# Score pieces of the A and B prompt attention put on TensorE two at a time, with four score banks and two shared by values and transposes

## The chip, the cores and the metric

One core of one Trainium2 chip. The metric is the device time of one execution in microseconds; three runs are taken and their median is told. TensorE is PE in the profile (PEld its weight loads), VectorE DVE, ScalarE ACT, GpSimd POOL and SyncE SP, the queue that issues most DMAs.

## What is computed

One layer of a streaming encoder, on 1024 prompt rows and 8 x 16 sample rows of width 1024. Three branches read one input projection; their outputs are gated, merged and followed by a feed-forward block. The change touches the prompt's part of branches A (a band of 64-row chunks with a bias by distance, 8 heads of 64) and B (causal, with a forget gate in the logits, 8 heads of 64), and, through the banks, the memory branch M and the sample rows:

```python
qa, ka, va, qb, kb, vb, logf, qm, gates = project(xn, ...)
# A: every 64-row chunk of queries reads its own and 8 earlier chunks
s = jnp.einsum('bcqhd,bckhd->bchqk', qc, kband) * d ** -0.5 + rel_bias
o_a = jnp.einsum('bchqk,bckhd->bcqhd', softmax(where(valid, s, -inf)), vband)
# B: every query reads all keys up to itself
s = jnp.einsum('bqhd,bkhd->bhqk', qi, k) * scale + ci[..., :, None] - c[..., None, :]
o_b = jnp.einsum('bhqk,bkhd->bqhd', softmax(where(k_pos <= q_pos, s, -inf)), v)
h = sigmoid(g_a) * (o_a @ w_pa) + sigmoid(g_b) * (o_b @ w_pb) + sigmoid(g_m) * (o_m @ w_pm)
x = x + h @ w_o
x = x + (relu(rmsnorm(x) @ w_up) ** 2) @ w_down
```

## The kernel before, in words

Values in float32 that need more than one TensorE pass are split into a high and a low part, and a product is three matmuls: high by high, high by low, low by high. The program runs through the input projection (to about 410 us), the attention stages with other products between them (to about 1100 us), the rest of the merge, and then W_o and the feed-forward block (to the end).

The attention stages run one after the other, each a call of `attend` (L1798 to L1807): prompt A, samples A, prompt B, samples B, prompt M, samples M. In each a generator yields tasks, and `Plan.run` (L148) decides on the order in which they are put on the engines. A task is a pair `ready` and `emit` with a chain's name. The planner keeps a clock of its own for PE (`plan.now`) and estimates for the other engines; it looks at the first 12 tasks, emits the first whose `ready()` is not after its clock, one chain's tasks in order, and where none is ready it takes one step of a filler, `plan.fill` (L135). The filler (`gates`, then `merge`) is the gate and merge products, matmuls on the whole 128 x 128 array into the two banks `z`. What is emitted is kept in program order on each engine, so the chip runs the order that the planner made.

PSUM has eight banks, given out by kind (L1777): two for filler (`z`), two for transposes (`tp`), three for scores (`s`), one for values (`pv`). `plan.bank(k, m)` tells when m banks of a kind are free by the planner's estimate, `take` and `free` keep its books.

`prompt_ab` (L1091) handles both branches. Heads go in pairs p, queries in blocks of 128, and n = 0 to 31 counts blocks over the four pairs (A upwards from block 0, B downwards from block 7). For each n:

- `scores` (L1161) cuts the block's keys into pieces of up to 512 columns: one piece up to 512 keys, two above. For A the number of keys is 128, 256, 384, 512 and then 640 (384 + 256) for blocks 0 to 7, for B 128 to 1024. A piece is a task (L1193): it takes two banks, one per head, and issues six matmuls, three terms by two heads. The two heads stand in the upper and lower 64 rows of the array (`tile_position`), and run side by side. `soften` (L1174) is the eviction: one VectorE instruction adds the bias and finds the row's extreme, and frees the bank; behind the last piece come the exponential on ACT and the scaling by DVE or POOL.
- `transposes` (L1214) turns the probabilities of n - 2 by PE into the `tp` banks; ACT or DVE copies them out as `pt`.
- `values` (L1258), for every second n, multiplies them with V into the `pv` bank, the two heads in the two column halves of the array; `os` is the copy on its way to HBM.

The sample stages use the array in four column strips of 32 (`s<-kd,qb`, `pv<-vd,spt`); their keys `kd` and values `vd` come from HBM through SP's queue. So the array is used whole (filler, transposes, M), by row halves (scores of A and B), by column halves (values of A and B) or by column strips (samples).

Of the kernel before, what the change touches and what calls it, by code (L numbers as in the profile page):

```python
# [187 lines left out]
def tile_encoder(ctx: ExitStack, tc: tile.TileContext, i, o):  # L188
# [902 lines left out]
    def prompt_ab(b, pool):  # L1091
# [69 lines left out]
        def scores(n):  # L1161
# [31 lines left out]
            def piece(x, m):  # L1193
                def ready():
                    return max(kq[p], bias_at[2 * p], bias_at[2 * p + 1], plan.bank("s", 2),
                               0.0 if x or 2 * n + 2 - softs[0] <= NS else INF)

                def emit():
                    qh, ql, kh, kl = heads[p][:4]
                    ks, qc, ps = slice(k0 * P + x, k0 * P + x + m), slice(blk * P, (blk + 1) * P), []  # L1200
                    for e in range(2):
                        if x == 0:
                            ss_[n, e] = tl(pool, (P, WK), tag="s", bufs=NS)
                        ps.append((plan.take("s"), tl(psum["s"], (P, 512), tag="s")))
                    for j, (q, k) in enumerate(((qh, kh), (qh, kl), (ql, kh))):
                        for e in range(2):
                            r = slice(64 * e, 64 * e + 64)
                            pe.matmul(ps[e][1][:, :m], q[r, qc], k[r, ks], start=j == 0, stop=j == 2, tile_position=(64 * e, 0))
                    for e in range(2):
                        plan.spawn(soften(e, ps[e][1], ps[e][0], x, m, x + m == nkey))  # L1210
                return ready, emit
            return [(*piece(x, m), ("s", n)) for x, m in pieces]
# [45 lines left out]
        def values(n):  # L1258
# [23 lines left out]
            def ready():  # L1282
                return max([vb[p], plan.bank("pv")] + [summed[x].get(e, INF) for x in (n - 1, n) for e in range(2)])

            def emit():
                bk = plan.take("pv")
                pv, vd = tl(psum["pv"], (P, 512), tag="pv")[:, 0:256], heads[p][4]
# [12 lines left out]
        plan.spawn(biases())  # L1300
        for n in range(32 + 4):
# [4 lines left out]
            if n < 32:  # L1306
                yield from scores(n)

    def prompt_m(pool):
# [98 lines left out]
        def values(n):  # L1408
# [11 lines left out]
            def ready():  # L1420
                return max(at["l", n], at["l", n - 1], at["in", 0], plan.bank("pv"))

            def emit():
                bk = plan.take("pv")
# [335 lines left out]
    def begin(gen):  # L1760

        for t in gen:
            plan.t = max(plan.t, t)
# [484 lines left out]
```

## Time and profile before

| | |
|---|---|
| median of 3 runs | 2029.59 us (2027.34 to 2035.56) |
| profiled execution, its own time | 2028.52 us |
| span of its trace | 2026.7 us |
| PE busy | 1968.0 us, 97% |
| DVE busy | 1233.7 us, 61% |
| ACT busy | 942.6 us, 47% |
| POOL busy | 524.8 us, 26% |

The profiled execution is 1.8 us longer than its span, and 1.1 us below the median. Matmuls are pipelined: a matmul's length in the trace runs into the next one's, so what one costs the queue is read from the distance of two starts. Time with nothing to wait for that the profile shows stands as "issue". Line numbers are those of the kernel before; L203 and L215 are the helpers that issue every ACT, DVE, POOL or SP instruction and every matmul, L222 the transposes.

### The profile page before, as it was taken

To read this page: it belongs to the slowest core of one execution; us is meant where nothing else is said; L and a number is where in the kernel's file an instruction comes from. 1 tells how busy PE (TensorE), PEld (TensorE's weight loads), DVE (VectorE), ACT (ScalarE), POOL (GpSimd) and SP (SyncE) were. 2 spreads that over 40 slices of the span, in tenths; PEclk is the share of its full clock that TensorE was granted. 3 is DMA by queue.
4 is the path that set the end of the run, shared out by engine and by line. 5 is a ranking of instruction groups with operands and counts; after the bars stand their busy time and mean duration, and the time that the engine had idled before them with its cause. 6 is when DMAs were issued, how large, how long until landed. Compare 5 with 4: busy or idle time off the path is not lost. (4 is left out here: it accounts for less than half of the span.)

```text
span 2026.7 us, 33952 instructions
## 1 busy us (share of the span) xinstructions
PE 1968.0 (97%) x12338; PEld 1710.5 (84%) x12338; DVE 1233.7 (61%) x2320; ACT 942.6 (47%) x1827; POOL 524.8 (26%) x587
## 2 busy tenths in 40 slices
PE   8999999899999999999998999989999999999999
PEld 8887888777778887787897987889999997888887
DVE  7776657666523655522575752785666565785775
ACT  6645556466633455533452222554444454453332
POOL 3343424233211234311122210244444331000000
PEclk9999999999999999999998999999999999999999
DMA  8556455642278333278657553134434359663463
GB/s 265 158 157 184 117 169 159 204 131 92 78 217 281 118 102 107 67 237 280 189 187 270 154 162 110 58 125 162 145 126 147 131 167 321 188 201 106 129 195 127
DMA packets 223910, 330.54 MB, mean 163 GB/s; under 512 B 32358, under 2 KB 109303, under 8 KB 223743
## 3 DMA queue, kind: packets, MB, share of 16 engines
q1 hardware_dynamic: 166600, 270.44, 42.1%
q10 hardware_dynamic: 57142, 57.93, 8.7%
q8 instruction: 97, 1.59, 0.3%
q14 instruction: 71, 0.57, 0.1%
HBM read 243.11 MB, written 85.18 MB: 162 GB/s over the span
## 5 line engine op out<-in xcount | busy, mean ns | idle before, releaser
L1849 PE MATMUL b<-r 128*128 128x512 f32 (+2 forms) x2200 | 456.7, 356 | 5.8 <-DVE r L203 3.2
L1849 PEld LDWEIGHTS b<-r 128*128 128x128 f32 x2200 | 378.8, 189 | 64.1 <-DVE r L203 4.6
L203 ACT ACTIVATE r<-fa 128x512 fp32r<-128x512 f32 (+4 forms) x264 | 212.8, 816 | 327.5 <-PE b L1849 278.0
L203 DVE TENSOR_TENSOR r<-fa,r 128x512 fp32r<-128x512 f32 (+4 forms) x264 | 275.5, 1055 | 137.9 <-ACT r L203 133.7
L215 PE MATMUL z<-hi,whi 128*128 128x384 f32 x960 | 321.2, 366 | 9.4 <-ACT hi L203 4.0
L1849 PE MATMUL b<-r,r 128*128 128x320 f32 (+1 forms) x1928 | 287.5, 299 | 5.2 <-DVE r L203 5.1
L1849 PEld LDWEIGHTS b<-r,r 128*128 128x128 f32 x1928 | 270.7, 190 | 7.0 <-DVE r L203 7.0
L215 PE MATMUL z<-hi,wlo 128*128 128x384 f32 x768 | 261.5, 341 | 0.2
L203 POOL TENSOR_TENSOR fa<-fa 128x512 f32<-128x512 f32 x114 | 166.0, 1463 | 238.8 <-ACT fa L203 135.4
L215 PEld LDWEIGHTS z<-hi,whi 128*128 128x128 f32 x960 | 180.3, 192 | 42.0 <-issue 23.3
L215 PE MATMUL z<-wa,hi 128*128 128x512 f32 (+1 forms) x732 | 203.7, 365 | 6.7 <-ACT hi L203 5.0
L215 PE MATMUL z<-lo,whi 128*128 128x384 f32 x576 | 194.9, 338 | 0.0
L215 PEld LDWEIGHTS z<-wa,hi 128*128 128x128 f32 x732 | 128.8, 192 | 27.6 <-ACT hi L203 5.4
L203 ACT ACTIVATE s<-s,nm 128x256 f32<-128x256 f32 (+8 forms) x180 | 121.4, 678 | 60.4 <-DVE nm L203 58.6
L215 PEld LDWEIGHTS z<-hi,wlo 128*128 128x128 f32 x768 | 146.8, 191 | 0.9 <-DVE wlo L203 0.9
L203 POOL TENSOR_SCALAR s<-s,ri 128x256 f32<-128x256 f32 (+8 forms) x105 | 77.0, 738 | 265.8 <-DVE ri L203 219.0
L203 DVE CUSTOM_DVE_ANT_0 s<-s,bias 128x384 f32<-128x384 f32 (+4 forms) x144 | 71.0, 526 | 100.5 <-PE s L215 100.0
L215 PE MATMUL z<-wa,lo 128*128 128x512 f32 (+1 forms) x366 | 130.2, 359 | 0.0
L215 PEld LDWEIGHTS z<-lo,whi 128*128 128x128 f32 x576 | 109.9, 191 | 0.0
L222 PE MATMUL tp<-ident,s 128*128 128x128 f32 (+1 forms) x680 | 102.2, 276 | 1.2 <-POOL s L203 1.2
L203 DVE TENSOR_TENSOR fa<-b,fa 128x256 f32<-128x256 f32 (+1 forms) x160 | 70.8, 450 | 52.4 <-PE b L1849 38.1
L203 DVE TENSOR_TENSOR wa<-rw,wa 128x512 fp32r<-128x512 f32 (+1 forms) x102 | 67.8, 687 | 56.3 <-ACT wa L203 56.3
(223 smaller groups left out, 3149.2 us busy)
## 6 DMA issues: line engine op xcount, KB each, us to landing
td<-fa SPq DMA_DIRECT2D x112, 256.0 KB
rw<-in_w_in SPq DMA_DIRECT2D x104, 256.0 KB
fa<-td SPq DMA_DIRECT2D x80, 256.0 KB
fa<-in_w_down SPq DMA_DIRECT2D x76, 256.0 KB
fa<-in_w_up SPq DMA_DIRECT2D x32, 512.0 KB
tg<-tg ACTq DMA_DIRECT2D x72, 192.0 KB
th<-tg SPq DMA_DIRECT2D x72, 192.0 KB
wst<-in_w_g ACTq DMA_DIRECT2D x48, 256.0 KB
```

The lines of the kernel that those rows point to most:

```text
L203: ins = f(*a, **k)
L215: ins = nc.tensor.matmul(out, lhsT, rhs, **k)
L222: ins = nc.tensor.transpose(*a)
L1849: pin(nc.tensor.matmul(ps, lh, rh, **k))
```

## The change

A score task is now one or two pieces, `together`. Its `ready` asks for two banks per piece, so for four with two pieces, and it emits the pieces one behind the other: twelve matmuls. B puts the pieces of one block together (one or two). A gathers pieces over the blocks until there are two: blocks 0 and 1, blocks 2 and 3, and the two pieces of each further block. The banks are given out anew: four for scores, and none of its own for values, which take one of the two `tp` banks, in the prompt's and the samples' stages alike.

```diff
@@ -1190,26 +1190,35 @@
                     yield from exp_norm(s[:, :nkey], s[:, :nkey], nkey, nm, pool)
                     done[n, e] = plan.t
 
-            def piece(x, m):
-                def ready():
-                    return max(kq[p], bias_at[2 * p], bias_at[2 * p + 1], plan.bank("s", 2),
-                               0.0 if x or 2 * n + 2 - softs[0] <= NS else INF)
-
-                def emit():
-                    qh, ql, kh, kl = heads[p][:4]
-                    ks, qc, ps = slice(k0 * P + x, k0 * P + x + m), slice(blk * P, (blk + 1) * P), []
+            def begin(x, m, heads):
+
+                qh, ql, kh, kl = heads[:4]
+                ks, qc, ps = slice(k0 * P + x, k0 * P + x + m), slice(blk * P, (blk + 1) * P), []
+                for e in range(2):
+                    if x == 0:
+                        ss_[n, e] = tl(pool, (P, WK), tag="s", bufs=NS)
+                    ps.append((plan.take("s"), tl(psum["s"], (P, 512), tag="s")))
+                for j, (q, k) in enumerate(((qh, kh), (qh, kl), (ql, kh))):
                     for e in range(2):
-                        if x == 0:
-                            ss_[n, e] = tl(pool, (P, WK), tag="s", bufs=NS)
-                        ps.append((plan.take("s"), tl(psum["s"], (P, 512), tag="s")))
-                    for j, (q, k) in enumerate(((qh, kh), (qh, kl), (ql, kh))):
-                        for e in range(2):
-                            r = slice(64 * e, 64 * e + 64)
-                            pe.matmul(ps[e][1][:, :m], q[r, qc], k[r, ks], start=j == 0, stop=j == 2, tile_position=(64 * e, 0))
-                    for e in range(2):
-                        plan.spawn(soften(e, ps[e][1], ps[e][0], x, m, x + m == nkey))
-                return ready, emit
-            return [(*piece(x, m), ("s", n)) for x, m in pieces]
+                        r = slice(64 * e, 64 * e + 64)
+                        pe.matmul(ps[e][1][:, :m], q[r, qc], k[r, ks], start=j == 0, stop=j == 2, tile_position=(64 * e, 0))
+                for e in range(2):
+                    plan.spawn(soften(e, ps[e][1], ps[e][0], x, m, x + m == nkey))
+            return [(p, n, x, m, begin) for x, m in pieces]
+
+        def together(pieces):
+
+            p = pieces[0][0]
+            last = max(n for _, n, _, _, _ in pieces)
+
+            def ready():
+                return max(kq[p], bias_at[2 * p], bias_at[2 * p + 1], plan.bank("s", 2 * len(pieces)),
+                           0.0 if 2 * last + 2 - softs[0] <= NS else INF)
+
+            def emit():
+                for _, _, x, m, begin in pieces:
+                    begin(x, m, heads[p])
+            return ready, emit, ("s", last)
 
         def transposes(n):
 
@@ -1280,11 +1289,11 @@
                 store(oT[b][p * P:(p + 1) * P, g * 256:(g + 1) * 256], os, 128)
 
             def ready():
-                return max([vb[p], plan.bank("pv")] + [summed[x].get(e, INF) for x in (n - 1, n) for e in range(2)])
+                return max([vb[p], plan.bank("tp")] + [summed[x].get(e, INF) for x in (n - 1, n) for e in range(2)])
 
             def emit():
-                bk = plan.take("pv")
-                pv, vd = tl(psum["pv"], (P, 512), tag="pv")[:, 0:256], heads[p][4]
+                bk = plan.take("tp")
+                pv, vd = tl(psum["tp"], (P, 512), tag="tp")[:, 0:256], heads[p][4]
                 for m, (kb, a, z) in enumerate(plan_):
                     u, r = divmod(kb - low(g), UK)
                     for e in range(2):
@@ -1298,13 +1307,18 @@
 
         plan.spawn(prepare(0))
         plan.spawn(biases())
+        waiting = []
         for n in range(32 + 4):
             if 0 <= n - 2 < 32:
                 yield from transposes(n - 2)
             if n - 3 >= 0 and n % 2 == 0:
                 yield from values(n - 3)
             if n < 32:
-                yield from scores(n)
+                waiting += scores(n)
+
+                if len(waiting) == 2 or b == "b":
+                    yield together(waiting)
+                    waiting = []
 
     def prompt_m(pool):
         mkp = tuple(tl(pool, (P, 4, NMEM), F32R, tag=f"mk{s}", bufs=1) for s in "hl")
...
@@ -1575,11 +1589,11 @@
         def values(n):
 
             def ready():
-                return max(at["T", n, 512], at["T", n, P], at["V", n], plan.bank("pv"))
+                return max(at["T", n, 512], at["T", n, P], at["V", n], plan.bank("tp"))
 
             def emit():
-                bk = plan.take("pv")
-                pv = tl(psum["pv"], (P, 512), tag="pv")
+                bk = plan.take("tp")
+                pv = tl(psum["tp"], (P, 512), tag="tp")
                 for k in range(5):
                     for pr in range(4):
                         pe.matmul(pv[32 * pr:32 * pr + 32, 0:P], pts[n][k][:, 32 * pr:32 * pr + 32], vv[n][k][:, pr * P:(pr + 1) * P],
...
@@ -1774,7 +1788,7 @@
     in_order.clear()
     prj.close()
     att = ExitStack()
-    plan.bufs = dict(z=2, tp=2, s=3, pv=1)
+    plan.bufs = dict(z=2, tp=2, s=4)
     att.enter_context(banks(**plan.bufs))
 
     def fillers():
```

**On PE, prompt B, first pair of heads.** The second block's score piece in the program before and the products behind it (`s` scores of the two heads, `z` filler):

```order
L215 MATMUL s_7513<-kh_7278,qh_7280 128x512
L215 MATMUL s_7515<-kh_7278,qh_7280 128x512
L215 MATMUL s_7513<-kl_7279,qh_7280 128x512
L215 MATMUL s_7515<-kl_7279,qh_7280 128x512
L215 MATMUL s_7513<-kh_7278,ql_7281 128x512
L215 MATMUL s_7515<-kh_7278,ql_7281 128x512
L215 MATMUL z_7472<-hi_144_212,whi_7429 128x384
L215 MATMUL z_7472<-lo_151_219,whi_7429 128x384
L215 MATMUL z_7472<-hi_144_212,wlo_7430 128x384
```

The same block in the changed program:

```order
L215 MATMUL s_7603<-kh_7374,qh_7376 128x512
L215 MATMUL s_7605<-kh_7374,qh_7376 128x512
L215 MATMUL s_7603<-kl_7375,qh_7376 128x512
L215 MATMUL s_7605<-kl_7375,qh_7376 128x512
L215 MATMUL s_7603<-kh_7374,ql_7377 128x512
L215 MATMUL s_7605<-kh_7374,ql_7377 128x512
L215 MATMUL s_7612<-kh_7374,qh_7376 128x384
L215 MATMUL s_7613<-kh_7374,qh_7376 128x384
L215 MATMUL s_7612<-kl_7375,qh_7376 128x384
L215 MATMUL s_7613<-kl_7375,qh_7376 128x384
L215 MATMUL s_7612<-kh_7374,ql_7377 128x384
L215 MATMUL s_7613<-kh_7374,ql_7377 128x384
```

The six score matmuls of 512 columns are followed at once by the six of the block's second piece (384 columns), which stood twelve products further on; filler stands ahead of and behind the twelve.

**On PE, prompt A, the first group of values.** Before (`pt` turned probabilities, `vd` the values):

```order
L215 MATMUL z_4203<-hi_143_211,wlo_4031 128x384
L215 MATMUL pv_4235<-pt_4112,vd_3839 64x256
L215 MATMUL pv_4235<-pt_4113,vd_3839 64x256
L215 MATMUL pv_4235<-pt_4112,vd_3839 64x128
L215 MATMUL pv_4235<-pt_4113,vd_3839 64x128
L215 MATMUL s_4246<-kh_3835,qh_3837 128x384
L215 MATMUL s_4248<-kh_3835,qh_3837 128x384
L215 MATMUL s_4246<-kl_3836,qh_3837 128x384
L215 MATMUL s_4248<-kl_3836,qh_3837 128x384
```

In the changed program:

```order
L215 MATMUL z_4235<-lo_146_214,whi_4027 128x384
L215 MATMUL z_4235<-hi_143_211,wlo_4028 128x384
L215 MATMUL tp_4257<-pt_4113,vd_3836 64x256
L215 MATMUL tp_4257<-pt_4114,vd_3836 64x256
L215 MATMUL tp_4257<-pt_4113,vd_3836 64x128
L215 MATMUL tp_4257<-pt_4114,vd_3836 64x128
L222 MATMUL tp_4269<-ident_203,s_4129 128x128 x3
L215 MATMUL z_4235<-hi_143_211,whi_4027 128x384
L215 MATMUL z_4235<-lo_147_215,whi_4027 128x384
```

The values' output is a `tp` tile in place of `pv`, and what follows is a transpose into the other `tp` bank and filler, where a score piece followed directly.

**On SP, the loads of the A samples.** Before (`kd` keys, `vd` and `v` values):

```order
L203 DMA vd_6670<-in_cav 128x512 x4
L203 DMA kd_6694<-in_cak 128x512 x4
L203 DMA kd_6747<-in_cak 128x512 x4
L203 DMA v_1240_6344<-out_va 16x512
L203 DMA vd_6813<-in_cav 128x512 x4
L203 DMA kd_6833<-in_cak 128x512 x4
L203 DMA v_1238_6342<-out_va 16x512
```

In the changed program:

```order
L203 DMA vd_6773<-in_cav 128x512 x4
L203 DMA kd_6800<-in_cak 128x512 x4
L203 DMA kd_6850<-in_cak 128x512 x4
L203 DMA kd_6907<-in_cak 128x512 x4
L203 DMA v_1252_6447<-out_va 16x512
L203 DMA vd_6934<-in_cav 128x512 x4
L203 DMA v_1250_6445<-out_va 16x512
```

A load of keys has moved ahead of the values of a sample before it; the loads ahead of these rows stand as they did.

## Rows read from the trace of the kernel before

**Rows 1.** The page, part 1: busy time, share of the span and instructions per engine.

```profile
PE 1968.0 (97%) x12338; PEld 1710.5 (84%) x12338; DVE 1233.7 (61%) x2320; ACT 942.6 (47%) x1827; POOL 524.8 (26%) x587
```

**Rows 2.** Windows: stretch, then busy time and instructions per engine, PEclk, DMA share, GB/s.

```profile
410.00:585.00 175.00, 175.00 (x1278) 141.41 (x1277) 99.48 (x344) 102.48 (x264) 52.76 (x73) 1.00 0.36 110
...
650.00:865.00 215.00, 215.00 (x1515) 176.44 (x1506) 120.73 (x357) 113.90 (x262) 72.26 (x112) 1.00 0.32 103
865.00:965.00 100.00, 93.87 (x844) 81.67 (x841) 27.98 (x87) 31.75 (x77) 14.59 (x35) 0.98 0.82 259
```

**Rows 3.** Tile `qh`: count, min/median/max ns, first and last start, then shapes.

```profile
L215 PE MATMUL s<-kh,qh x192: 322/439/503, 410.5 to 863.6; 64*128 64x384 f32 x80, 64*128 64x256 f32 x56, 64*128 64x512 f32 x40, 64*128 64x128 f32 x16
```

**Rows 4.** Timeline of PE, 769 to 774 us: start, length, instruction.

```profile
769.17 0.60 PE L222 MATMUL tp<-ident,s 128*128 128x128 f32 x4
769.53 0.42 PE L215 MATMUL z<-hi,whi 128*128 128x384 f32 x1
...
771.17 0.38 PE L222 MATMUL tp<-ident,s 128*128 128x128 f32 x2
771.31 0.42 PE L215 MATMUL z<-hi,whi 128*128 128x384 f32 x1
771.57 0.34 PE L215 MATMUL z<-lo,whi 128*128 128x384 f32 x1
771.75 0.33 PE L215 MATMUL z<-hi,wlo 128*128 128x384 f32 x1
772.01 0.51 PE L215 MATMUL s<-kh,qh 64*128 64x512 f32 x2
772.35 0.40 PE L215 MATMUL s<-kl,qh 64*128 64x512 f32 x2
772.58 0.40 PE L215 MATMUL s<-kh,ql 64*128 64x512 f32 x2
772.92 0.44 PE L215 MATMUL z<-hi,whi 128*128 128x384 f32 x1
773.20 0.34 PE L215 MATMUL z<-lo,whi 128*128 128x384 f32 x1
773.37 0.33 PE L215 MATMUL z<-hi,wlo 128*128 128x384 f32 x1
```

**Rows 5.** Timeline of PE, 599 to 601 us, around column-tiled products.

```profile
599.04 0.34 PE L215 MATMUL z<-hi,wlo 128*128 128x384 f32 x1
599.31 1.08 PE L215 MATMUL pv<-vd,spt 128*32 128x128 f32 x32
...
600.54 0.45 PE L215 MATMUL z<-hi,whi 128*128 128x384 f32 x1
600.82 0.34 PE L215 MATMUL z<-lo,whi 128*128 128x384 f32 x1
```

**Rows 6.** Weight loads (PEld), 410 to 865 us, by line and shape; idle time at the end.

```profile
L215 PEld LDWEIGHTS z<-hi,whi 128*128 128x128 f32 x414 | 78.4, 189 | 22.6 <-issue 19.0
...
L215 PEld LDWEIGHTS s<-kh,qh 64*128 64x128 f32 x192 | 17.9, 183 | 19.9 <-issue 17.3 <-DVE pt L203 0.7 <-DVE s L203 0.5
```

**Rows 7.** Who PE waited for, 410 to 1100 us: us in total, times, longest.

```profile
PE z L215 <- ACT hi L203: 4.0, 3, 1.5
PE s L215 <- DMA kd<-in_cak: 3.4, 3, 2.6
PE s L215 <- DMA kd<-in_cmk: 2.7, 1, 2.7
```

**Rows 8.** Windows around one stall, 600 to 611 us.

```profile
607.20:610.60 3.40, 3.40 (x15) 2.62 (x10) 1.46 (x7) 0.83 (x2) 0.72 (x2) 0.50 0.93 348
```

**Rows 9.** DVE, 410 to 865 us, by line and shape: score evictions.

```profile
L203 DVE CUSTOM_DVE_ANT_0 s<-s,bias 128x512 f32<-128x512 f32 x32 | 20.8, 689 | 26.1 <-PE s L215 26.1
...
L203 DVE CUSTOM_DVE_ANT_0 s<-s,bias,nm 128x512 f32<-128x512 f32 x8 | 5.7, 749 | 5.5 <-PE s L215 5.5
```

**Rows 10.** ACT, 410 to 865 us, by line and shape: the values' eviction.

```profile
L203 ACT ACTIVATE os<-pv 128x256 f32<-128x256 f32 x25 | 9.6, 384 | 32.2 <-PE pv L215 32.2
```

More of the change, by code (lines that the diff above doesn't have):

```diff
@@ L1420, in ready @@
             def ready():
-                return max(at["l", n], at["l", n - 1], at["in", 0], plan.bank("pv"))
+                return max(at["l", n], at["l", n - 1], at["in", 0], plan.bank("tp"))
             def emit():
-                bk = plan.take("pv")
-                pv = tl(psum["pv"], (P, 512), tag="pv")
+                bk = plan.take("tp")
+                pv = tl(psum["tp"], (P, 512), tag="tp")
                 mm3(pv, lambda k: tuple(m[:, k, h * P:(h + 1) * P] for m in mvp),
@@ L1577, in ready @@
             def ready():
-                return max(at["T", n, 512], at["T", n, P], at["V", n], plan.bank("pv"))
+                return max(at["T", n, 512], at["T", n, P], at["V", n], plan.bank("tp"))
             def emit():
-                bk = plan.take("pv")
-                pv = tl(psum["pv"], (P, 512), tag="pv")
+                bk = plan.take("tp")
+                pv = tl(psum["tp"], (P, 512), tag="tp")
                 for k in range(5):
@@ L1716, in emit @@
             def emit():
-                bk = plan.take("pv")
-                pv = tl(psum["pv"], (P, 2, P), tag="pv")
+                bk = plan.take("tp")
+                pv = tl(psum["tp"], (P, 2, P), tag="tp")
                 for e in range(2):
@@ L1725, in emit @@
                 plan.spawn(out(pv, bk))
-            return lambda: max(at["t", n], at["v", 2 * n], at["v", 2 * n + 1], plan.bank("pv")), emit, ("v", n)
+            return lambda: max(at["t", n], at["v", 2 * n], at["v", 2 * n + 1], plan.bank("tp")), emit, ("v", n)
         def turn(n):
```

## The prediction

> **What bounds the kernel now.** I read the page's busy times first: TensorE is busy for 97% of the span, the next engine, VectorE, for 61% [rows 1]. A share of 97% can still hide stages with other limits, so the windows come next. The two stretches in which the changed code runs are the prompt's A attention (410 to 585 us) and B attention (650 to 865 us). In both PE is busy for the whole length, 175.00 of 175.00 and 215.00 of 215.00 us, at full granted clock, with DVE at 57% and 56% and the DMA engines at about a third [rows 2]. So these 390 us are set by TensorE alone: what shortens its queue shortens them. The list of who waited for whom says the same. Over 410 to 1100 us it has only twelve entries for PE, the largest 4.0 us in total; none of them lies inside the two windows, and none is a score matmul waiting for a bank that VectorE still held. The waits stand in the sample and memory stages, mostly for keys from HBM [rows 7].
>
> A busy PE is not a PE at its peak, and the timeline shows what the busy time contains [rows 4]. Inside a run of whole-array products, starts are 0.17 to 0.18 us apart for 384 columns. Around a score piece they are not. I read the starts one after the other, for a piece of 512 columns whose two heads run side by side:
>
> - last whole product to first score, 771.75 to 772.01: 0.26 instead of 0.17, **0.09** more;
> - first score pair to second, 772.01 to 772.35: 0.34, where the next step inside the same piece (772.35 to 772.58) takes 0.23, **0.11** more;
> - third pair to the first whole product, 772.58 to 772.92: 0.34 instead of 0.23, **0.11** more;
> - that product to the next, 772.92 to 773.20: 0.28 instead of 0.17, **0.11** more.
>
> Together 0.42 us per excursion into the halved array and back, half of it on each boundary. It depends little on the width of the piece, since it is added to each step and not to each column. The weight loads give a second measure: from 410 to 865 us the PEld engine sat idle with nothing that the profile shows to wait for, 17.3 us before the scores' first loads and 19.0 us before the first loads of whole products [rows 6]. There are 192 first-term matmuls [rows 3], two heads per piece, so 96 pieces; 36.3 / 96 = 0.38 us. That lies a little off, since some of the second sum belongs to other kinds of run. I take 0.40 us per excursion, 0.20 per boundary.
>
> **The change part by part.** *Scores in pairs.* The order of the two programs shows that the change does what it says: before, 96 score runs of 6 matmuls each; now 40 runs of 12 and 16 of 6 (B's single-piece blocks). The matmuls are the same in number, shape and operands; only their neighbours differ. 40 excursions are gone, 80 boundaries.
>
> *The planner's other moves.* With four score banks asked for at once, the planner fills more time with gate products, and in the sample stages it splits the column-tiled products into 35 runs where there were 30. Entering and leaving such a run costs about the same as a score run: 599.04 to 599.31 is 0.27, and the first product behind it, 600.54 to 600.82, takes 0.28 [rows 5]. That gives 10 boundaries back. Before, a score run and a run of values stood side by side nine times, which saved a return to the whole array; now four times. That gives 5 back. Counted over the whole order: 307 boundaries before, 242 now, 65 fewer. 65 x 0.20 = **13.0 us less**, all of it on PE's own queue, which sets the time there. More transposes now stand apart between products, but both use the whole array: the two transposes and the product at 771.17 to 771.57 take 0.40 us, where two transposes at 0.11 (the difference of 0.36 for four and 0.14 for two, halved) and a product at 0.17 make 0.39 [rows 4]. Nothing for these.
>
> *The first step of the second piece.* Twelve in a row do not occur before. At the least, its first pair follows as inside a piece, 0.23 us at 512 columns; at the most it pays the 0.11 of a first pair again, 40 x 0.11 = 4.4 us. I take nothing, since the nearest row is a step between two pairs in the same mode, with new weights, and that is what it is.
>
> *Four banks at once.* A pair of pieces now starts only when all four banks are clear, where one piece needed two of three. Evictions of 512 columns take 0.69 and 0.75 us on DVE [rows 9]. If all cover went, each of the 40 doubled runs would wait for two more evictions, about 1.4 us, 56 us in all. At the least it is nothing. I take nothing: DVE is idle for over 40% of both stretches [rows 2], PE never waited for such a bank before, and the planner puts other work between doubled runs: behind the doubled run that is shown from the changed order (512 and 384 columns) stand twelve products and eight transposes before the next, 12 x 0.17 + 8 x 0.11 = 2.9 us [rows 4]. Four evictions take at most 2 x 0.69 + 2 x 0.75 = 2.9 us, and the first starts while the second piece, some 0.8 us, is still on PE. If the planner's guess is late by a few tenths somewhere, PE stands that long.
>
> *Values in the transposes' banks.* There were two banks for transposes and one for values; now two for both. 32 value groups hold a bank for ACT's 0.38 us [rows 10]; if a transpose waited for each, 32 x 0.38 = 12 us. I take nothing: the planner asks for the bank before it issues and has filler to issue instead, so PE is covered as long as there is filler. There is: the gate and merge products go on well after the last attention matmul in both orders. Without that cover the 12 us would stand.
>
> *Other engines and queues.* The evictions are the same work; a few change between DVE and ACT. On SP the 833 issues are the same, with a few swapped in the sample stages: a key load goes ahead of a value load by one place. The stalled keys of the A samples (3.4 us [rows 7]) are queued further ahead and do not move. These stalls can shrink or grow by some us: at the least 3.4 us vanish, and with them the following 3.4 us at a granted clock of 0.50 [rows 8], worth 1.7 us; at the most as much is added when PE, earlier by a few us, meets the same loads.
>
> **The sum.** The profiled execution took 2028.5 us. 2028.5 - 13.0 = 2015.5. The median of the three runs, 2029.6, is 1.1 us above that execution, so I say **2016**.
>
> **The rivals.**
>
> 1. *VectorE becomes the bound in the doubled runs; slower than before.* Place: the 40 doubled runs. Four evictions in a row instead of two must end before the next doubled run. Price: up to 56 us, less the 13: 2073. It decides the sign from 13.0 / 40 = 0.33 us of waiting per doubled run, and the forecast of a slower kernel by over 0.5% from 23 / 40 = 0.6 us. For it: before, PE could start a piece while the third bank was still being read, and that overlap is gone. Against it: DVE's idle time and PE's list of waits, as said [rows 2, 7]. At half of the waits that would even things out, 6.5 us, the time is 2022, no change. The Trainium skill, page "TensorEngine Tiling (Array Packing)", section "PSUM Bottleneck", warns of this: a faster TensorE may leave the copy out of PSUM as the bound. The trace before shows no sign of it.
>
> 2. *The second piece pays its first weight load again.* The step between pieces costs 0.34 instead of 0.23. Then 13.0 - 4.4 = 8.6 us less: 2021, inside what a measurement can't tell. Against it: 772.35 to 772.58 [rows 4], where weights on the same rows of the array change without a gap. The Trainium skill, page "TensorE: Matmul & The Clock Gate", section "The mechanism", says that a weight load overlaps matmuls in flight only where the row group differs. By that rule this rival would hold; the row speaks against it, because head 0's second weights follow head 0's first in the same row group and no load is exposed.
>
> 3. *The sample stages take it back.* From 865 to 965 us the DMA engines are busy at 0.82 and PE stands for 6 us [rows 2]. PE reaches keys that come no sooner, and loses, say, that again: 13.0 - 6.1 = 6.9 us, 2023. Against it: the loads are issued when the attention before them ends, so they start earlier too.
>
> **How the numbers follow.** The likeliest, PE's saving as counted (2016): 0.70. Rival 1 in full: 0.05; in part (2022): 0.09. Rival 2: 0.07. Rival 3: 0.09. About 0.5%, 10 us, is what a measurement of this kernel can tell from no change, so faster means under 2019.4. The first case lies there; rivals 2, 3 and the partial 1 are no change, 0.25; slower is 0.05. The range takes in the vanishing stalls below (5 us, and 4 for the spread of the price per boundary and of the runs): 2007. Above it takes in rivals 2 and 3 and the partial 1: 2024. What is left out is the full rival 1 and odd mixtures.
>
> **What would show it.** In the profile after: starts inside a doubled run with one long step (0.34 at 512) and no second one at the seam; PEld idle by "issue" before `s<-kh,qh` down from 17.3 to about 10 us and before `z<-hi,whi` down too; the two attention windows still full, with PE waiting for no DVE. Wrong would be: waits of PE's scores for DVE's evictions, PE below full in these windows, or longer stalls for keys in the sample stages. If the time does not fall though the idle weight loads have gone, the saving was given back later, and the windows from 585 to 1190 us must show where.

## The result, and the profile after

The changed kernel takes 2010.68 us in the median (2004.36 to 2013.25, seven runs), the kernel before 2027.34 us beside it (2020.87 to 2035.56, seven runs): a ratio of 0.9921 [0.9907, 0.9935], 16.7 us less in the medians. The forecast was 2016 us and faster. Single executions of one kernel spread by up to 0.8%, so the medians carry the verdicts here. The profiled execution took 2010.68 us, 17.8 less than the one of before.

The page's busy time per engine. It answers to [rows 1]: the same 12338 matmuls, PE busy for 13.3 us less.

```profile
PE 1954.7 (97%) x12338; PEld 1712.1 (85%) x12338; DVE 1221.4 (61%) x2313; ACT 946.0 (47%) x1831; POOL 521.1 (26%) x590
```

The windows of after by stage (columns as in [rows 2]):

```profile
410.00:585.00 175.00, 173.35 (x1304) 148.53 (x1304) 98.56 (x345) 102.07 (x265) 51.24 (x74) 1.00 0.33 106
585.00:650.00 65.00, 62.65 (x669) 51.93 (x669) 19.45 (x66) 23.67 (x56) 8.17 (x16) 1.00 0.93 305
650.00:855.00 205.00, 204.96 (x1488) 173.60 (x1488) 112.59 (x352) 116.21 (x266) 75.99 (x116) 1.00 0.34 108
855.00:955.00 100.00, 93.73 (x835) 78.33 (x833) 26.28 (x80) 32.24 (x76) 16.70 (x36) 0.98 0.84 264
955.00:1050.00 95.00, 88.85 (x558) 84.23 (x558) 60.98 (x117) 48.28 (x126) 15.62 (x13) 0.95 0.57 176
1050.00:1092.00 42.00, 38.59 (x344) 31.70 (x342) 19.23 (x44) 9.60 (x25) 3.41 (x5) 0.88 0.82 298
1092.00:1175.00 83.00, 78.92 (x442) 76.04 (x441) 67.03 (x111) 28.95 (x54) 25.22 (x19) 1.00 0.57 177
```

The two prompt stages stay full but for 1.65 and 0.04 us, with DVE and DMA as in [rows 2]. From the first A score to the last B score it takes 442.1 us instead of 453.4: 11.3 us are gained by the end of B's scores. The stretch from there to the first memory score takes 128.0 instead of 127.7 us, and from that score to the last merge product 190.1 instead of 198.6, where the rest of the gain lies.

The timeline of PE through a doubled run of 512 columns (start, length, instruction). It answers to [rows 4]:

```profile
766.84 0.50 PE L215 MATMUL s<-kh,qh 64*128 64x512 f32 x2
767.17 0.39 PE L215 MATMUL s<-kl,qh 64*128 64x512 f32 x2
767.40 0.40 PE L215 MATMUL s<-kh,ql 64*128 64x512 f32 x2
767.63 0.40 PE L215 MATMUL s<-kh,qh 64*128 64x512 f32 x2
767.87 0.39 PE L215 MATMUL s<-kl,qh 64*128 64x512 f32 x2
768.10 0.40 PE L215 MATMUL s<-kh,ql 64*128 64x512 f32 x2
768.42 0.44 PE L222 MATMUL tp<-ident,s 128*128 128x128 f32 x2
```

The first step is 0.33 us, the last 0.32, and every one between them 0.23 to 0.24. The seam (767.40 to 767.63) is 0.23, like any inner step. So the second piece of a run pays nothing for its weight load.

The weight loads of after, 410 to 855 us, by line and shape (busy, mean ns, idle before and what ended it):

```profile
L215 PEld LDWEIGHTS z<-hi,whi 128*128 128x128 f32 x426 | 80.4, 189 | 11.4 <-issue 8.0 <-ACT kh L203 0.3
...
L215 PEld LDWEIGHTS s<-kh,qh 64*128 64x128 f32 x192 | 18.0, 184 | 10.8 <-issue 8.3 <-DVE ri L203 0.7 <-DVE pt L203 0.5
```

The idle "issue" time of [rows 6] has fallen from 19.0 to 8.0 us at the whole products and from 17.3 to 8.3 at the scores, together 20 us.

Who PE waited for, 410 to 1172 us (us in total, times, longest):

```profile
PE z L215 <- ACT hi L203: 8.0, 3, 3.6
PE z L215 <- ACT whi L203: 3.6, 2, 3.0
PE z L215 <- DVE th L203: 3.4, 4, 1.0
PE tp L222 <- ACT of L203: 1.4, 2, 1.1
PE tp L215 <- ACT spt L203: 1.2, 1, 1.2
PE s L215 <- DMA kd<-in_cak: 1.2, 2, 0.7
PE tp L222 <- ACT pt L203: 1.2, 1, 1.2
```

Against [rows 7], the memory keys `in_cmk` no longer hold PE up and the A keys do so for 1.2 instead of 3.4 us; the first merge products wait twice as long for `hi`, the split of the attention outputs loaded back from HBM (8.0, before 4.0), and the filler waits for weights (`whi`). No score matmul waits for a bank that DVE holds.

To separate PE's own work from its waits, I took every PE matmul's distance to the next start, its median in the trace of before for its kind, width and neighbours, and summed these steps over each kernel's order, from the first A score to the last merge product. What the trace took more is the rest: waits, and what is lost in the stretches in which the granted clock was 0.50. The table has both kernels and, ahead of their account, five of the experiments below. "Stands" is the time without any matmul on PE, ahead of and behind the first memory score; in brackets are second profiles of the two kernels.

| kernel | boundaries | queue steps, us | rest, us | stands ahead, us | behind, us | at clock 0.50, us | ratio (95%) |
|---|---|---|---|---|---|---|---|
| before | 307 | 731.1 | 48.5 (44.9) | 13.4 (10.5) | 13.3 (13.4) | 23.9 (20.5) | 1 |
| after | 242 | 717.5 | 42.7 (43.6) | 16.5 (14.7) | 6.9 (6.5) | 23.9 (23.9) | 0.9921 [0.9907, 0.9935] |
| e1_banks | 259 | 721.7 | 33.4 | 9.1 | 8.7 | 3.4 | 0.9916 [0.9898, 0.9934] |
| e2_split | 307 | 729.9 | 44.5 | 18.8 | 5.5 | 17.1 | 0.9956 [0.9942, 0.9969] |
| e3_join | 217 | 713.3 | 40.6 | 16.0 | 5.3 | 13.7 | 0.9909 [0.9892, 0.9927] |
| e5_shared | 309 | 731.3 | 30.9 | 10.7 | 5.2 | 6.8 | 0.9913 [0.9897, 0.9930] |
| e14_follow | 211 | 712.5 | 39.6 | 18.1 | 5.6 | 13.7 | 0.9885 [0.9866, 0.9904] |

65 boundaries fewer are 13.6 us of steps, 0.21 each. The rest of the gain is waits, 5.8 us between the first two profiles and 1.3 between the second two. A profile is one execution, and its rest carries that execution's luck: the one of e1_banks was 4.0 us below its kernel's median, the one of e2_split 4.2 above. From the end of the last merge product to the end of PE's work the kernels take 830 to 836 us (before 832, the fastest of all 832); nothing is given back there.

### The profile page after: what moved, and what is told of

Its sections match the earlier page's. It is cut to its first block, busy times and chain, and to the rows that moved or that the text cites. A ratio compares the mean times of both kernels' runs of the same rounds, so it can differ in the third digit from the quotient of the medians.

```text
span 2008.9 us, 33955 instructions
## 1 busy us (share of the span) xinstructions
PE 1954.7 (97%) x12338; PEld 1712.1 (85%) x12338; DVE 1221.4 (61%) x2313; ACT 946.0 (47%) x1831; POOL 521.1 (26%) x590
## 4 chain that ended last, share of the span: by engine, by line
PE 77%; DMA 10%; DVE 6%; ACT 2%; issue 2%; POOL 2%; SPq 1%; ACTq 0%; POOLq 0%; DVEq 0%
PE b L1863 36%; PE z L215 28%; PE tp L222 5%; PE tp L215 4%; PE s L215 4%; DMA wst<-in_w_g 2%; DMA th<-tg 1%; POOL fa L203 1%; DVE r L203 1%; DVE fa L203 1%; DVE lo L203 1%; DMA kd<-in_cak 1%; DMA fa<-in_w_up 1%; SPq L203 1%; DMA tg<-tg 1%
## 5 line engine op out<-in xcount | busy, mean ns | idle before, releaser
L222 PE MATMUL tp<-ident,s 128*128 128x128 f32 (+1 forms) x680 | 107.3, 277 | 1.7 <-ACT pt L203 1.2
L203 ACT ACTIVATE pt<-tp 128x256 f32<-128x256 f32 (+3 forms) x153 | 66.4, 454 | 80.6 <-PE tp L222 76.8
```

The source lines that it names most:

```text
L203: ins = f(*a, **k)
L222: ins = nc.tensor.transpose(*a)
```

## The experiments

**Two more profiles.** c1_before and c2_after are the two kernels again, unedited.

> The kernel before once more, for a second profile: how much of its waits in the sample and memory stages (585 to 650 and 865 to 1190 us, some 48 us over the queue's own steps in the first profile) stands in every execution. Theory (two thirds of the gain is the queue's, the rest is fewer or shorter waits in these stages in the new order): 40 to 55 us of waits again, in the same stages. Rival (the first profile of before was an unlucky one): waits lower by 8 us or more.

> The changed kernel once more, for a second profile. Theory: PE's queue again 13 to 14 us shorter than before, since its steps are the same in every execution; the waits to the end of the merge, 44 us in the first profile, anywhere from 33 to 48. Rival (the changed kernel's waits are as those of before): 48 to 52.

They took 2025.65 and 2013.76 us (one execution each). The queue's sum stays, since the orders are the same; the rest moves by 1 to 4 us from one profile to the next. That is how finely a single trace can be read.

**One piece at a time, with the new banks (e1_banks).** Four score banks and shared transposes stay, the doubling goes.

```diff
-                waiting += scores(n)
-
-                if len(waiting) == 2 or b == "b":
-                    yield together(waiting)
-                    waiting = []
+                for w in scores(n):
+                    yield together([w])
```

> The changed kernel's banks (four for scores, two shared by values and transposes), but every score piece a task of its own again, which asks for two free banks. In the order that the planner makes of it, 21 pairs of pieces still stand one behind the other (54 runs of 6, 21 of 12) and TensorE changes its tiling 259 times, against 307 before and 242 changed. Theory (a boundary costs 0.20 us of PE's queue, nothing else matters): 48 boundaries fewer than before, 9.6 us less, ratio to before 0.9953; 3.4 us above the changed kernel. Rival (the gain comes from asking for pairs, that is from the planner's other order of filler and loads): near the time before, ratio 1.000. Rival (the gain comes from the banks alone, by fewer waits): as fast as the changed kernel, 0.992, though with more boundaries.

Measured: 0.9916, 2008.20 us, as fast as after. So asking for four banks at once isn't needed for the gain. But this is no clean removal of the doubled runs either: with four banks clear, the planner puts two single pieces behind each other by itself (21 runs of twelve matmuls, 54 of six), so 48 of the 65 boundaries stay away.

**The pair cut apart (e2_split).** Everything as in after, with one filler step between the two pieces, so that each pays its own way into the halved array and back.

```diff
-                for _, _, x, m, begin in pieces:
+                for j, (_, _, x, m, begin) in enumerate(pieces):
+                    if j:
+                        plan.fill()
                     begin(x, m, heads[p])
```

> The changed kernel, but between the two pieces of a task the planner takes one step of filler, three whole-array products. Banks, pairs and evictions stay as in the changed kernel; the order has 96 score runs of 6 matmuls and 307 boundaries, exactly as many as before. Theory (boundaries alone): the queue's gain of 13.0 us is gone, ratio to before 0.999 to 1.001, apart from what the waits in the sample and memory stages do by some us. Rival (banks or the planner's order give the gain, not the array's changes of tiling): the ratio stays near 0.992.

Measured: 0.9956, 2015.88 us, 307 boundaries as in before. Its weight loads from 410 to 880 us:

```profile
L215 PEld LDWEIGHTS z<-hi,whi 128*128 128x128 f32 x434 | 82.1, 189 | 18.5 <-issue 16.7
...
L215 PEld LDWEIGHTS s<-kh,qh 64*128 64x128 f32 x190 | 17.7, 183 | 20.0 <-issue 13.1 <-DVE nm L203 4.7 <-DVE ri L203 1.2
```

The idle "issue" time comes back with the boundaries: 16.7 and 13.1 us. Against after the queue is 12.4 us longer, the ratios differ by 7 us (the intervals allow 3 to 11), and the two profiled executions by 9. So putting the boundaries back costs time, and by the ratios not quite half of the gain is lost with them. The filler step between the pieces also moves filler (1779 products stand ahead of the first memory score, 1734 in after), so the 7 us are not the boundaries alone. With the boundaries of before, however, the kernel is still 0.44% faster than before: something else in the change helps.

**B gathers as A does (e3_join).** Also B's single pieces wait for a second one.

```diff
-                if len(waiting) == 2 or b == "b":
+                if len(waiting) == 2:
```

> The changed kernel, but B gathers single pieces over blocks as A does, so that its blocks 3 and 2, and 1 and 0, go together: 48 runs of 12, 217 boundaries. Theory (0.20 us per boundary): 25 fewer than the changed kernel, 5.0 us less, ratio to before 0.9895. Rival (a block's evictions in B wait for the mask that POOL adds to the bias behind the block ahead, and PE waits for the banks): PE waits for DVE in the last blocks of B, up to the 8 runs times about 1 us, ratio 0.992 to 0.994.

Measured: 0.9909, 2007.06 us. 25 boundaries fewer than after, 4.2 us of steps; the median is 3.6 us lower (2.4 by the ratios). The sign and size fit, but the intervals overlap, so a gain over after is not shown.

**More work on VectorE (e4_evict).** To see how much margin the four banks leave, each eviction of a doubled run gets a copy of the same piece ahead of it on DVE, which holds the bank for as long again. The copy is superfluous (the eviction overwrites it), and the planner's books don't know of it.

```diff
                 s, bias = ss_[n, e], heads[p][5][e]
+                if more:
+                    vec.tensor_copy(s[:, x:x + m], ps[:, :m])
```

> The changed kernel, with one more VectorE copy ahead of each eviction of a doubled run (160 copies, 0.3 to 0.7 us each, about 2.2 us per run), of which the planner is not told. The output is the reference's. In the trace of the changed kernel PE starts a doubled run 1.1 us or more after the last eviction that it needs (median 2.2). Theory (VectorE has that margin and no more): about half of the 40 runs overrun it, by 0.5 us on average over all, so 15 to 30 us slower than the changed kernel, with PE waiting for DVE before score runs. Rival (the four banks are a bound already, each added us is paid in full): 40 x 2.2 = 88 us slower. Rival (ample slack): no difference.

Measured: 1.0146, 2053.28 us, some 44 us more than after. DVE over 410 to 910 us, the four shapes of the copy:

```profile
L203 DVE COPY s<-s 128x384 f32<-128x384 f32 x72 | 39.6, 550 | 14.8 <-PE s L215 14.8
...
L203 DVE COPY s<-s 128x512 f32<-128x512 f32 x32 | 21.9, 686 | 8.9 <-PE s L215 8.9
...
L203 DVE COPY s<-s 128x256 f32<-128x256 f32 x48 | 20.0, 418 | 0.0
...
L203 DVE COPY s<-s 128x128 f32<-128x128 f32 x8 | 2.3, 288 | 2.1 <-PE s L215 2.1
```

and PE's waits in the same stretch:

```profile
PE tp L222 <- POOL s L203: 10.8, 7, 3.2
PE s L215 <- DVE nm L203: 6.5, 12, 0.8
```

160 copies, 83.8 us in all; about half of it is paid. Here DVE does hold score banks (`s <- DVE nm`), which it never does in after. In after's trace the doubled runs start at least 1.06 us after the last eviction that they need, 2.2 us in the median; the copies add 1.4 to 2.7 us of DVE for each run. So the margin is at least about 1 us per run and the changed kernel lies inside it. Only 6.5 us stand as waits for a bank; more reaches PE further down the chain, as transposes that wait for scaled probabilities (`tp <- POOL s`, 10.8 us where after has 0.3).

**The shared banks alone (e5_shared).** The kernel before, single pieces and three score banks; values of all stages go into the transposes' two banks, and the eighth bank is used by nobody.

```diff
-    plan.bufs = dict(z=2, tp=2, s=3, pv=1)
+    plan.bufs = dict(z=2, tp=2, s=3)
...
-                bk = plan.take("pv")
+                bk = plan.take("tp")
```

> The kernel before with one part of the change alone: values and transposes share two banks; scores keep three banks and go one piece at a time, and one bank stays unused. 309 boundaries against 307. Theory (what the kernel with split pairs gained without fewer boundaries, a ratio of 0.9956, comes from the planner's other order in the sample and memory stages, which sharing the banks brings about): ratio 0.994 to 0.998. Rival (it comes from the fourth score bank): ratio 1.000. Rival (sharing two banks costs waits of transposes for the copies of values): slower than before, 1.001 to 1.004.

Measured: 0.9913, 2009.91 us: as much as the whole change, with 309 boundaries. Its windows:

```profile
410.00:587.00 177.00, 177.00 (x1274) 143.40 (x1275) 102.08 (x345) 101.50 (x260) 53.35 (x75) 1.00 0.32 103
587.00:652.00 65.00, 64.10 (x671) 52.12 (x669) 19.90 (x68) 23.03 (x56) 6.93 (x15) 1.00 0.93 308
652.00:867.00 215.00, 215.00 (x1516) 177.04 (x1516) 114.74 (x352) 118.01 (x269) 79.63 (x120) 1.00 0.32 103
867.00:967.00 100.00, 91.70 (x822) 79.06 (x821) 27.19 (x82) 30.37 (x72) 12.51 (x31) 0.98 0.84 267
967.00:1060.00 93.00, 91.52 (x585) 87.63 (x586) 66.95 (x119) 51.48 (x133) 23.65 (x20) 0.98 0.62 189
1060.00:1096.00 36.00, 33.00 (x304) 27.65 (x303) 15.46 (x36) 8.14 (x21) 5.78 (x7) 1.00 0.95 341
1096.00:1175.00 79.00, 76.78 (x456) 73.98 (x455) 62.11 (x108) 27.89 (x54) 20.54 (x16) 1.00 0.54 166
```

The prompt stages have their old length. From 967 us on PE stands for 1.48 + 3.00 + 2.22 = 6.7 us at a granted clock of 0.98 to 1.00; in after, from 955 us, for 6.15 + 3.41 + 4.08 = 13.6 us, with two windows at 0.95 and 0.88. From the first memory score to the last merge product it takes 177.4 us, after 190.1, before 198.6. The order shows what the sharing changed: 1779 filler matmuls stand ahead of the first memory score and 2136 ahead of the last sample matmul, in before 1734 and 2049. Asking for the shared bank, the planner finds it taken more often and fills (so its code reads; it was not counted); 45 products more ahead of the memory stage are 7.9 us at 0.175, and the queue behind is 7.8 us shorter (176.9 to 169.1). Of the 7.9 the earlier stages show 3.8 us as longer time against the first profile of before and 7.3 against the second, so at most some 4 us were waits there before. Behind the first memory score 21.2 us are gained, 7.8 of them steps that moved ahead, so some 13 us are waits. PE stands there for 5.2 us instead of 13.3, and it runs at a granted clock of 0.50 for 6.8 us in all instead of 23.9. That the moved filler is what shortens these waits is argued from the order and not shown.

The kernels with doubled runs can be read against this one as well. By their ratios after is 1.6 us slower than e5_shared, e1_banks 0.6 slower, e3_join 0.8 and e14_follow 5.7 faster, with 9.6 to 18.8 us of steps fewer. Only e14_follow's difference is clear of the noise, and barely. So on top of the shared banks the pairs' steps have hardly become time, except there.

**Three score banks outside the prompt (e6_three).** The planner's count of score banks is four in prompt A and B only.

```diff
+        plan.bufs["s"] = 4 if name in ("aa", "ab") else 3
```

> The changed kernel, but outside the prompt's A and B stages the planner uses three score banks, as before. 242 boundaries, as in the changed kernel. Theory (the fourth bank is of use in the doubled runs alone): ratio 0.990 to 0.994, as the changed kernel. Rival (the part of the gain that is not the queue's comes from the fourth score bank in the sample and memory stages): 0.995 to 0.997.

Measured: 0.9921, 2011.62 us, the same as after, with the same boundaries. The fourth score bank does nothing in the sample and memory stages.

**The planner believes the loads to be slower.** Three kernels with 270 instead of 350 KB per us in the planner's estimate of DMA: after (e10_slow), e3_join (e12_join_slow) and e5_shared (e13_shared_slow), to see whether more filler in the sample stages would give the pairs e5's small waits.

```diff
-        ... max(0.45, kb / (350 if queue == "dma" else 350))
+        ... max(0.45, kb / 270)
```

> The changed kernel with another estimate in the planner: its DMA queues at 270 KB per us in place of 350, so that it puts more filler ahead of work that waits for loads. 246 boundaries; by the queue's steps read from the trace of before, 720.0 us of TensorE steps from the first score to the end of the merge, 1.3 less than the changed kernel. Theory (the changed kernel gave back some 10 us as waits for loads in the sample and memory stages, where the sharing alone had 31 us of waits and the changed kernel 44): waits fall to 30 to 36 us, ratio to before 0.985 to 0.988. Rival (the stretch from the B samples to the memory stage lasts as long as its loads, whatever stands on PE): waits stay at 40 or more, ratio 0.990 to 0.993.

> The same estimate of 270 KB per us with the pairs of B gathered over blocks: 230 boundaries, 717.8 us of queue steps, 2.2 less than with the plain pairs. Theory: ratio 0.984 to 0.987, the fastest of all. Rival (loads set the stretch): 0.990 to 0.993.

> The same estimate with the shared banks alone, three score banks and single pieces: 326 boundaries, 736.1 us of queue steps, 16.1 more than with the pairs; from the end of the B samples to the end of the memory stages the filler stands at the same places as in the kernel with pairs and this estimate. Theory (a boundary costs 0.20 us wherever the waits are equal): 13 to 18 us slower than that kernel, ratio to before 0.992 to 0.996. Rival (the pairs' saving is always eaten by later waits, as between the shared banks alone, 0.9913, and the changed kernel, 0.9921): the same time as that kernel within 4 us.

Measured: 1.0046, 1.0044 and 1.0098, all slower than before; a miss. Among other moves, e10 spends 864 filler products by the end of the A samples where after has spent 735, 1830 ahead of the first memory score, and has too little left for the B samples. PE's waits in e10 from 410 to 1191 us:

```profile
PE z L215 <- ACT whi L203: 11.7, 3, 8.1
PE tp L222 <- POOL s L203: 8.8, 5, 3.1
PE tp L222 <- ACT of L203: 4.6, 7, 1.3
PE tp L215 <- ACT spt L203: 4.0, 3, 2.9
```

The rest in the table's sense is over 60 us in e10 and in e13. One thing can still be read. From the memory stage on e10 and e13 have their filler in the same places (1830 products ahead of the first memory score in both), with 246 and 326 boundaries: 16.1 us of steps apart, and 11.8 us in the medians (2034.96 and 2046.78). In this pair of kernels the doubled runs are worth most of their steps.

**The values right behind a pair (e14_follow).** e3_join, and a value group that is ready is put directly behind the pair, before the filler, which saves a return to the whole array.

```diff
                 for _, _, x, m, begin in pieces:
                     begin(x, m, heads[p])
+                after_scores[:] = [f for f in after_scores if not f()]
...
+            def follow():
+                if not state["done"] and ready() <= plan.now:
+                    put()
+                return state["done"]
+            after_scores.append(follow)
...
```

> The pairs gathered over blocks in B too, and values that are ready are put right behind a pair's twelve matmuls: 211 boundaries, 716.2 us of TensorE steps from the first score to the end of the merge, 20.4 less than with the shared banks alone (736.6). From the B samples on the filler stands where it stands with the shared banks alone (1779 filler matmuls ahead of the first memory score, 2136 ahead of the last sample matmul, in both), where the changed kernel has 1734 and 2082. Theory (the pairs' saving is kept where the filler stands so that the waits after the B samples stay at some 31 us; the changed kernel lost it by its place in the filler): ratio to before 0.981 to 0.985, the fastest of all. Rival (the stretch from the B samples to the end of the memory stage is set by loads, and what PE saves ahead of it comes back as waits there): 0.988 to 0.992, waits of 40 us or more.

Measured: 0.9885 [0.9866, 0.9904], 2001.35 us: the fastest of all, 9 us below after (7 by the ratios). Its windows:

```profile
410.00:585.00 175.00, 173.00 (x1304) 148.55 (x1303) 100.92 (x344) 102.45 (x266) 51.46 (x75) 1.00 0.33 106
585.00:650.00 65.00, 62.31 (x669) 52.37 (x669) 19.75 (x67) 22.52 (x55) 8.17 (x16) 1.00 0.92 308
650.00:855.00 205.00, 203.28 (x1492) 174.47 (x1491) 110.42 (x336) 116.22 (x264) 73.09 (x110) 1.00 0.34 107
855.00:955.00 100.00, 90.97 (x831) 78.69 (x829) 28.73 (x93) 33.44 (x83) 15.25 (x37) 0.98 0.83 264
955.00:1050.00 95.00, 92.39 (x587) 87.95 (x588) 68.22 (x120) 51.09 (x133) 22.30 (x19) 0.96 0.61 189
1050.00:1086.00 36.00, 32.99 (x298) 27.93 (x298) 15.63 (x36) 8.10 (x21) 4.00 (x5) 0.95 0.94 340
1086.00:1164.00 78.00, 75.41 (x450) 72.71 (x449) 59.89 (x104) 26.73 (x51) 20.17 (x16) 1.00 0.53 157
```

B's last score comes 443.7 us behind A's first, 442.1 in after. From 955 us PE stands for 2.61 + 3.01 + 2.59 = 8.2 us, near e5's 6.7, and it too has 1779 filler products ahead of the first memory score. The queue is 18.6 us shorter than before. But ahead of 955 us it stands for 2.00 + 2.69 + 1.72 + 9.03 = 15.4 us, where e5 stands for 9.2 ahead of 967: the two gains add up in part.

## Why the prediction was right, and where not

**Scores in pairs: the steps were right, their worth in time is shown only in part.** 65 boundaries at 0.20 us were to give 13.0 us; the steps summed over the changed order give 13.6, and the idle weight loads fell by 20 us. The fall shows where the price was seen [rows 4, 6]. That it becomes time is borne out twice: e2_split puts the boundaries back and loses 7 us, and e10 and e13 differ by 12. Against e5_shared, however, the pairs and the fourth bank bring nothing (0.9921 and 0.9913). Pairs without the shared banks were not run, so what they give by themselves is not measured.

**The first step of the second piece: right.** It costs nothing; the second rival is refuted. The seam is 0.23 us and an inner step the same. The Trainium skill, page "TensorE: Matmul & The Clock Gate", section "The mechanism", says that a weight load overlaps matmuls in flight only where the row group differs. The trace of after doesn't bear this out: within one run each head's next weights go to the row group that it is using, and the steps behind the first stay at 0.23 to 0.24 us.

**Four banks at once: right.** The first rival, VectorE as the bound, didn't come; no score matmul waits for an eviction. e4_evict, with 1.4 to 2.7 us more of VectorE work per run, shows that the mechanism exists when the margin, 1.06 us at the least, is overrun; where between them it begins was not measured.

**The planner's other moves, and the sample stages.** The count of boundaries held. The third rival, PE earlier at loads that come no sooner, came in part. The wait for the memory keys has gone, since their load is issued 10.8 us ahead of its first use where it was 7.4. But ahead of the first memory score PE stands for 16.5 us instead of 13.4 (second profiles 14.7 and 10.5): some 3 to 4 us, below the 6.1 of its price. The keys are not what it waits for: `in_cak` and `in_cbk` hold it up for 2.2 us, before 5.2. The filler's own inputs are. After, 875 to 982 us:

```profile
PE z L215 <- ACT hi L203: 5.6, 2, 3.6
PE z L215 <- ACT whi L203: 3.6, 2, 3.0
```

and before, 884 to 992 us, where `whi` is not among the waits:

```profile
PE z L215 <- ACT hi L203: 2.8, 2, 1.5
```

Being earlier is not the whole cause either: e2_split stands for 18.8 us there, though its last B score comes 462.1 us behind the first A score and not sooner than in before.

**Values in the transposes' banks: this step failed.** "I take nothing" was the term, with 12 us of loss as its bound. Alone, the sharing is worth 17.6 us (0.9913), as much as the whole change, and all of it in waits: 48.5 and 44.9 us of rest became 30.9. I looked at the sharing only as a wait for a bank, and not at what the planner does while it holds back: it moves filler ahead. The total came out within 6 us because the two effects don't add: in after the rest is 12 to 13 us longer than in e5_shared, in e3_join and e14_follow 9 to 10, and so the change as a whole gives its 13.6 us of steps and a few us of waits. That the sum came so near the measured time with this term at nothing is luck: had both been added, the forecast would have been some 30 us, and wrong. Of the 5.3 us by which the time was missed, 2.3 lie in the kernel before, which took 2027.3 us beside it and not 2029.6.

**Other engines and queues.** A gain or loss of about 5 us by stalls was allowed for, and a gain of 1 to 6 came: 6 to 7 us less of standing behind the first memory score, 3 to 4 more ahead of it. How much of it is the filler's new places is not shown.

**What stays open** is why after, e3_join and e14_follow keep those 9 to 13 us. The table shows where they lie. The four kernels that ask for four banks at once (after, e2_split, e3_join, e14_follow) stand for 15 to 19 us ahead of the first memory score, e1_banks and e5_shared, which ask for two, for 9 to 11. Behind it all stand for 5 to 9 us, but after is at a clock of 0.50 for 10.2 us there and e5_shared not at all. The waits of after name the start of the merge (`z <- ACT hi`, 8.0 us, none in e5_shared). After also has its filler ahead of the memory stage where before had it (1734). e1_banks, e2_split, e3_join, e5_shared and e14_follow have 1767 to 1782 there, and from the first memory score to the last merge product they take 177 to 184 us instead of 190 to 199. But e2_split is among them and is slower as a whole, and pushing filler ahead by the planner's load estimate made it worse. The place of the filler was not changed by itself.

## What to carry to other kernels

Price a change of the array's layout from the starts in the timeline, count such changes over the whole order, and put work of the same layout together; here each cost 0.21 us. Where a planner issues filler, a resource that is made scarcer is not only a wait to be bounded: it moves the filler, and in this kernel making it scarcer was worth by itself as much as the whole change. Test the parts of a change alone before crediting one, since here one part worth 14 us by its steps and one that alone gave 17.6 us made 16.7 together.

## What the runs showed of the hardware that was not expected

- Passing from whole array to row halves and back costs on four steps, about 0.09 to 0.11 us each, and nothing in between, for one piece or two and with a weight load at every matmul. The other layouts cost less: by the median steps in the traces of all runs 0.30 us for column halves, there and back, and 0.33 for column strips, against 0.40; the prediction took column strips to cost about as much. The Trainium skill, page "TensorEngine Tiling (Array Packing)", section "Key Properties", says that changing the tiling mode drains TensorE, with no price; the steps at a run's start and end, 0.33 and 0.32 us against 0.23, fit that.
- Waits cost more than their length. After's granted clock falls to 0.50, which is 1.2 of 2.4 GHz, for 10.2 us behind a wait of 2.04 us for `hi` (another of 3.56 us lies in the stretch), and again for 10.2 us behind one of 2.42:

```profile
965.80:976.00 10.20, 6.40 (x18) 5.49 (x19) 2.92 (x5) 4.91 (x9) 1.31 (x1) 0.50 0.59 192
1054.60:1064.80 10.20, 8.96 (x34) 5.75 (x35) 4.36 (x9) 2.08 (x6) 0.48 (x1) 0.50 1.05 408
```

  They are what the 0.95 and 0.88 of its windows from 955 to 1092 us are made of. e5_shared, with half the waits there, keeps 0.98 to 1.00. From the first A score to the last merge product the clock is at 0.50 for 23.9 us in before and 6.8 in e5_shared, whose steps are the same within 0.2 us.
